# An eighth seven-product pair per layer, and two of its weight sums made by adding DMAs, in a two-layer mLSTM and retention encoder

## The chip, the cores and the metric

The kernel runs on one core of a Trainium2 chip. The metric is the device time of one execution in microseconds, lower is better; the time of the kernel before is the median of three runs.

## What is computed

Two layers, one after the other, each on 256 tokens of 2048 features in float32. A layer normalises its input, multiplies it by one wide weight matrix, and cuts the product into twelve parts. Two token mixers work on them: a bidirectional mLSTM and a bidirectional retention. Each mixer's result is normalised per head, multiplied by a SiLU gate, projected, and merged with the other under a sigmoid gate. An output projection and a residual add close the layer.

```python
def hybrid_layer(x, ...):
    h = rmsnorm(x, norm_w)
    proj = jnp.einsum('bsd,de->bse', h, w_in)
    (q_m, k_m, v_m, z_m, o_m, g_m, q_r, k_r, v_r, z_r, gate_m, gate_r) = jnp.split(proj, ...)
    ...
    h_m = jax.nn.sigmoid(split_heads(o_m, NH_M)) * h_m            # mLSTM scans, both directions
    u_m = head_rmsnorm(h_m, m_norm_w) * jax.nn.silu(z_m)
    ...
    u_r = head_rmsnorm(h_r, r_norm_w) * jax.nn.silu(z_r)          # retention scans, both directions
    mix = jax.nn.sigmoid(jnp.concatenate([gate_m, gate_r], axis=-1) + b_mix)
    y = (mix[..., :D_MODEL] * jnp.einsum('bse,ed->bsd', u_m, w_proj_m)
         + mix[..., D_MODEL:] * jnp.einsum('bse,ed->bsd', u_r, w_proj_r))
    return x + jnp.einsum('bsd,de->bse', y, w_out)
```

## The kernel before

**Weights and matmuls.** Tokens make two tiles of 128 (`t` = 0, 1), and 2048 features of a weight part make four blocks `b` of 512 columns. A weight block streams in from device memory in chunks of 128 x 1024 float32 (512 KB: two k-tiles of 128 rows by 512 columns). `wload` (line 251) puts a chunk into one of seven `raw` buffers, on the queue of the engine SP. Float32 products are made of three passes: `wsplit` has ScalarE round the chunk to `whi` (line 262) and VectorE subtract it, which leaves `wlo` (line 263); `mm3` then multiplies high by high, high by low and low by high (lines 271 to 273). `whi` and `wlo` come from a ring of twelve buffers, six pairs. A plain block (`gemm`, lines 332 to 351) is eight chunks, each used by 12 matmuls of 512 columns, six for each token tile.

**Side pairs.** `seven` (line 411) computes two blocks of one weight part together for both token tiles, in seven half-sized products where eight would do it plainly: the two token tiles by the two halves of the 2048 input features are one 2 x 2 matrix, the two halves of the features by the two blocks of columns the other. Each of the seven products takes four chunks (index `i`), six matmuls a chunk. The weight operand of a product is a quarter of the pair (`r11`, `r12`, `r21`, `r22`) or a sum of quarters. Product p5 uses r11+r12, p6 uses that plus r22 (kept in a big tile, `keep`), p7 uses r12+r22, and p4 uses the kept sum plus r21. Every one of these sums is a VectorE addition of 128 x 1024: `wsum` (line 268) for p5, p7 and p4, line 445 for p6. `middle` and `end` add the products together; `finish` (line 818) applies the gate function (a sigmoid or SiLU) to each 128 x 512 result and spills it to device memory. In each layer seven pairs are made so: the mLSTM output gate (`om`, two pairs), the merging gates (`gm` and `gr`, two pairs each), and blocks 0 and 1 of the retention's SiLU gate (`zr`).

**How the side work is woven in.** The items of the side pairs stand in one list, with weights (1.6 for a product with a VectorE sum, 0.5 without). After each chunk of a plain block, `side_chunk` puts in as many items as keep the list even over `20 * NCK` chunks, which is twenty blocks. `side_need` runs the list forward until a given result has been spilled. So through most of a layer TensorE alternates between a plain chunk and side products. Four places wait for side results: the blocks of `z_m` (name `zm`), the mLSTM projection (`pj`, with `gm`), the retention's gate and projection (with `gr`), and the next step.

**Spills and fetches.** A spill (line 99) is a DMA of 256 KB on the queue of the engine POOL. A fetch (line 105) is one on SP's queue, the same queue that the weights use, and it is in order: what stands behind a waiting issue waits too. A fetch lands in a 128 x 512 buffer of a ring of seven (`t512`), which the gate results (`c`, `z`), fetches and other temporaries share. Names in the trace end in `_b` for a fetched tile: `hm_b` is the mLSTM's output and `so_b` its sigmoid gate.

**The stage of `zm`.** For block `b` of four, `gated` fetches hm and om for both token tiles, multiplies them (VectorE) and sums the squares (ScalarE, which writes over `so_b`); meanwhile the plain block of `zm` runs; then the SiLU of it is multiplied in (`z<-hm_b,rstd_m,z`) and `um_chunk` transposes and splits the result, which is the left operand of `pj`.

**What sets the order.** The program is written in Python order and a list scheduler sorts each engine's instructions: `high_priority(offset=AHEAD)` (800) or `URGENT` (1600) lifts an instruction above those of the surrounding code. Each engine then runs its own list strictly in order. Functions given to `later` are generators that `run_later` steps, one step a chunk, from the third chunk on (`lead=3`).

Of the kernel before, what the change touches and what calls it, by code (L numbers as in the profile page):

```python
# [16 lines left out]
P = 128  # L17
D = 2048
# [43 lines left out]
def encoder_kernel(ctx: ExitStack, tc: tile.TileContext, x, x_t, positions, w_main, w_qk0, w_qk1, b_mgate, vecs, b_mix,  # L62
# [321 lines left out]
    def sums_of_operand(ht_hi, ht_lo, make_items):  # L384
# [24 lines left out]
        side_start(make_items(s_hi=s_hi, s_lo=s_lo, keep=bigt("keep", 4)), 20 * NCK)  # L409

    def seven(l, xop, s_hi, s_lo, keep, blk, finish):
# [17 lines left out]
        def p1(i):  # L429
            if i == 0:  # L430
                for name in "abcd":
                    st["ps_" + name] = bank("s" + name)
            load("r11", 0, i)
# [30 lines left out]
        def p2(i):  # L464
            if i == 0:
                for name in "acd":
                    st["ps_" + name] = bank("r" + name)
            load("r21", 0, HC + i)
            load("r22", 1, HC + i)
            product(st["ps_a"], lambda kt: xop(0, HK + kt), st["r21"], i, True, True)  # L470
# [293 lines left out]
    for l in range(DEPTH):  # L764
# [54 lines left out]
        def side_items(l=l, xop=xop, rs=rs, s_hi=None, s_lo=None, keep=None):  # L819
            def finish_with(kind, b0):  # L820
                def finish(t, n, src, own):
                    sg = t512(kind) if own is None else own
                    b = b0 + n
                    if kind in ("om", "zr"):
                        sca.activation(out=sg, in_=src, func=AF.Sigmoid if kind == "om" else AF.Silu, scale=rs[t])
                    else:
                        bm = row("bm")
                        mc = (0 if kind == "gm" else D) + b * NB
                        with tc.high_priority(offset=AHEAD):
                            nc.scalar.dma_start(out=bm, in_=b_mix[l:l + 1, mc:mc + NB].broadcast_to([P, NB]))  # L830
# [4 lines left out]
                return finish  # L835
            items = []
            for kind, base, b in (("om", B_O_M, 0), ("om", B_O_M, 2), ("gm", B_GATE, 0), ("gm", B_GATE, 2),
                                  ("zr", B_Z_R, 0), ("gr", B_GATE + NBLK, 0), ("gr", B_GATE + NBLK, 2)):
                items += seven(l, xop, s_hi, s_lo, keep, base + b, finish_with(kind, b))
# [52 lines left out]
        um = []  # L892
# [13 lines left out]
        def um_chunk(ev, b):  # L906
            um.append(transpose_split(ev, b, None, None, (l, V_MN)))

        for b in range(NBLK):
            side_need(("om", l, b, 1))  # L910
            side_need(("om", l, b, 0))
            hs = []
            ss_m = sm.tile([P, NT], F32, name="ss_m")
            later(gated, b, hs, ss_m)
            ps = gemm(xop, wmain(l, B_Z_M + b), "zm")
            while len(hs) <= NT:
                run_later()
            rstd_m = hs[NT]
            ev = []
            for t in range(NT):  # L920
                z = t512("z")
                sca.activation(out=z, in_=ps[t], func=AF.Silu, scale=rs[t])
                vec.scalar_tensor_tensor(out=z, in0=hs[t], scalar=rstd_m[:, t:t + 1], in1=z,
                                               op0=ALU.mult, op1=ALU.mult)
                ev.append(z)
            later(um_chunk, ev, b)
# [6 lines left out]
        for b in range(NBLK):  # L933
            ps = gemm(uop, wmain(l, B_PROJ_M + b), "pj")
            for t in range(NT):
                side_need(("gm", l, b, t))
                sg = fetch(("gm", l, b, t), "gm_b")
# [5 lines left out]
        def ur_chunk(b, zs):  # L943
            ev = []
            hrs = [fetch(("hr", l, 2 * b + k), "hr_b") for k in range(2)]
            for t in range(NT):
                z = fetch(("zr", l, b, t), "z_b") if zs is None else zs[t]
# [6 lines left out]
            if zs is None:  # L954
                yield
# [27 lines left out]
        for b in range(NBLK):  # L983
            if b == 2:
# [4 lines left out]
                later(y_chunk, None, 1)  # L989
            ps = gemm(rop, wmain(l, B_PROJ_R + b), "pj", lead=2)  # L990
            ev = []
            for t in range(NT):
                side_need(("gr", l, b, t))
                sg = fetch(("gr", l, b, t), "gr_b")
                ym = fetch(("ym", l, b, t), "ym_b")
# [184 lines left out]
```

## Time and profile before

| | |
|---|---|
| median of three runs | 2194.8 us (2194.19, 2194.8, 5458.12) |
| profiled execution, its own time | 2194.46 us |
| its span, first to last instruction | 2192.4 us |
| mean granted TensorE clock | 0.995 |
| TensorE (PE) busy | 2154.0 us, 98% |
| VectorE (DVE) busy | 1813.4 us, 83% |
| ScalarE (ACT) busy | 1304.3 us, 59% |
| data moved by DMA | 518.25 MB, mean 236 GB/s |

The profile's times come from one execution; 2.1 us of it lie outside the span. Busy shares are averages over the whole span. A timeline row gives start and duration of an instruction, and in square brackets how long the engine stood idle before it and what released it. Rows of stretches (the view by windows) give, for each engine, busy time and the count of instructions, and then the granted clock of TensorE, the busy share of the DMA engines and their GB/s.

### The profile page before, as it was taken

The numbers are of one execution on the slowest core, as the hardware profiler recorded it, in microseconds if no ns is written. First come the engines' busy times: TensorE is split into PE (matmuls) and PEld (weight loads), VectorE is DVE, ScalarE is ACT, GpSimd is POOL, SyncE is SP. The second block draws the span as 40 slices with busy tenths as digits, with TensorE's granted clock in tenths as the row PEclk, the third lists the DMA queues.
The fourth block names the chain that finished last, engine by engine and source line by source line (L and its number), as shares of the span: only waits on it lengthen the run. The fifth ranks groups of instructions, "written<-read, shape, count | busy, mean of one in ns | idle before, by whom it ended". The sixth has DMA issues, their size and how long they took to land.

```text
span 2192.4 us, 28486 instructions
## 1 busy us (share of the span) xinstructions
PE 2154.0 (98%) x10024; PEld 1809.9 (83%) x10024; DVE 1813.4 (83%) x2327; ACT 1304.3 (59%) x1627; POOL 66.9 (3%) x130
## 2 busy tenths in 40 slices
PE   7999999999999999999999999999999999999998
PEld 7988888888778888888899888888887788888887
DVE  6997898897898998985578778989978989889854
ACT  6745466656775656564457555665567656565543
POOL 0000000000000000000000000000000000000000
PEclk9999999999999999999999999999999999999999
DMA  8645577767777887887656456776777778878963
GB/s 277 213 150 190 191 236 236 229 229 241 241 241 264 280 283 258 271 295 276 221 168 208 164 185 210 236 234 216 240 247 239 255 255 292 280 252 277 326 223 125
DMA packets 161071, 518.25 MB, mean 236 GB/s; under 512 B 19616, under 2 KB 22176, under 8 KB 160928
## 3 DMA queue, kind: packets, MB, share of 16 engines
q1 hardware_dynamic: 143552, 471.98, 65.4%
q0 software_dynamic: 9600, 31.46, 3.6%
q10 hardware_dynamic: 7776, 13.00, 2.0%
q8 instruction: 78, 1.28, 0.2%
q14 instruction: 65, 0.53, 0.1%
HBM read 482.81 MB, written 33.55 MB: 236 GB/s over the span
## 4 chain that ended last, share of the span: by engine, by line
issue 48%; PE 42%; DVE 3%; DMA 3%; POOL 2%; ACT 1%; SPq 0%; ACTq 0%; POOLq 0%; DVEq 0%
PE pj L272 3%; PE pj L273 3%; PE pj L271 3%; DVE wlo L263 2%; PE vm L271 1%; PE vm L272 1%; PE wo L273 1%; PE wo L272 1%; PE wo L271 1%; PE vr L271 1%; PE vr L272 1%; PE qr L271 1%; PE vm L273 1%; PE qr L273 1%; PE vr L273 1%
## 5 line engine op out<-in xcount | busy, mean ns | idle before, releaser
L262 ACT CAST whi<-raw 128x1024 fp32r<-128x1024 f32 (+2 forms) x832 | 844.6, 1034 | 608.1 <-DVE raw L268 147.7
L263 DVE TENSOR_TENSOR wlo<-raw,whi 128x1024 fp32r<-128x1024 f32 (+2 forms) x832 | 981.0, 1200 | 214.7 <-ACT whi L262 200.1
L272 PE MATMUL pj<-wlo,u_hi 128*128 128x512 f32 x512 | 199.4, 390 | 0.6 <-DVE wlo L263 0.5
L271 PE MATMUL pj<-whi,u_hi 128*128 128x512 f32 x512 | 199.9, 391 | 0.0
L273 PE MATMUL pj<-whi,u_lo 128*128 128x512 f32 x512 | 199.3, 389 | 0.0
L262 ACT CAST whi<-keep 128x1024 fp32r<-128x1024 f32 x112 | 117.7, 1051 | 60.0 <-PE qr L272 12.8
L263 DVE TENSOR_TENSOR wlo<-keep,whi 128x1024 fp32r<-128x1024 f32 x112 | 136.4, 1218 | 15.7 <-ACT whi L262 15.1
L268 DVE TENSOR_TENSOR raw<-raw 128x1024 f32<-128x1024 f32 x112 | 136.4, 1218 | 0.8
L271 PE MATMUL qk<-whi,ht_hi 128*128 128x384 f32 (+2 forms) x320 | 113.7, 357 | 10.5 <-ACT whi L262 10.5
L272 PE MATMUL qk<-wlo,ht_hi 128*128 128x384 f32 (+2 forms) x320 | 113.4, 354 | 1.0 <-DVE wlo L263 1.0
L272 PEld LDWEIGHTS pj<-wlo,u_hi 128*128 128x128 f32 x512 | 96.1, 188 | 21.0 <-DVE wlo L263 1.5
L273 PE MATMUL qk<-whi,ht_lo 128*128 128x384 f32 (+2 forms) x320 | 113.0, 353 | 0.0
L273 PEld LDWEIGHTS pj<-whi,u_lo 128*128 128x128 f32 x512 | 96.1, 188 | 20.0
L271 PEld LDWEIGHTS pj<-whi,u_hi 128*128 128x128 f32 x512 | 96.0, 188 | 20.0 <-ACT whi L262 0.4
L272 PE MATMUL zm<-wlo,ht_hi 128*128 128x512 f32 x256 | 100.0, 391 | 1.0 <-DVE wlo L263 0.9
L271 PE MATMUL vm<-whi,ht_hi 128*128 128x512 f32 x256 | 100.3, 392 | 0.0
L273 PE MATMUL vm<-whi,ht_lo 128*128 128x512 f32 x256 | 100.2, 391 | 0.0
L271 PE MATMUL vr<-whi,ht_hi 128*128 128x512 f32 x256 | 100.1, 391 | 0.0
L271 PE MATMUL qr<-whi,ht_hi 128*128 128x512 f32 x256 | 100.1, 391 | 0.0
L272 PE MATMUL vm<-wlo,ht_hi 128*128 128x512 f32 x256 | 100.0, 391 | 0.0
L271 PE MATMUL zm<-whi,ht_hi 128*128 128x512 f32 x256 | 100.0, 392 | 0.0
L272 PE MATMUL vr<-wlo,ht_hi 128*128 128x512 f32 x256 | 99.8, 390 | 0.0
(313 smaller groups left out, 4664.6 us busy)
## 6 DMA issues: line engine op xcount, KB each, us to landing
raw<-in_w_main_dram SPq DMA_DIRECT2D x776, 512.0 KB, 5.0
raw<-in_w_qk_dram SPq DMA_DIRECT2D x48, 384.0 KB, 3.2
bm<-in_b_mix_dram ACTq DMA_DIRECT2D x32, 256.0 KB, 4.4
raw<-in_w_qk_dram SPq DMA_DIRECT2D x15, 400.0 KB, 5.2
hm<-hm POOLq DMA_DIRECT2D x16, 256.0 KB, 4.6
om<-c POOLq DMA_DIRECT2D x16, 256.0 KB, 3.5
hr<-hr POOLq DMA_DIRECT2D x16, 256.0 KB, 5.7
gm<-c POOLq DMA_DIRECT2D x16, 256.0 KB, 4.7
```

Of the source, the lines that this page charges most:

```text
L262: nc.scalar.copy(out=whi, in_=raw)
L263: nc.vector.tensor_tensor(out=wlo, in0=raw, in1=whi.bitcast(F32), op=ALU.subtract)
L268: nc.vector.tensor_tensor(out=dst, in0=a, in1=b, op=ALU.add)
L271: nc.tensor.matmul(out=ps, lhsT=xh, rhs=whi, start=first, stop=False)
L272: nc.tensor.matmul(out=ps, lhsT=xh, rhs=wlo, start=False, stop=False)
L273: nc.tensor.matmul(out=ps, lhsT=xl, rhs=whi, start=False, stop=last)
```

## The change

It has three parts. First, blocks 0 and 1 of the mLSTM's SiLU gate become an eighth side pair in each layer, spilled as `zm` and fetched where they are used. The loop over `zm` then has two plain blocks (2 and 3); beside each, `gated` runs for two heads, b and b-2, and fetches all of its four tiles before the first multiply. The side list is spread over `18 * NCK` chunks. Second, the sums of p7 and p4 leave VectorE: p1 loads r22 as `t3` and POOL issues a DMA that adds r12 from device memory into it; p6 issues one that adds r21 into the kept sum. These are 64 DMAs of 512 KB a layer, on POOL's queue. p5's sum now goes into the buffer of r12, since r11 is still read. Third, the bias rows of the merging gates (`bm`) are loaded by SP one step earlier, no longer by ScalarE's queue, and the fetches of `gm`, `ym` and `gr` stand ahead of the block that they gate.

```diff
-        side_start(make_items(s_hi=s_hi, s_lo=s_lo, keep=bigt("keep", 4)), 20 * NCK)
+        side_start(make_items(s_hi=s_hi, s_lo=s_lo, keep=bigt("keep", 4)), 18 * NCK)
...
             load("r12", 1, i)
-            load("r22", 1, HC + i)
+            load("t3", 1, HC + i)
+            with tc.high_priority(offset=AHEAD):
+                nc.gpsimd.dma_start(out=st["t3"], in_=wmain(l, blk + 1)(i), accum_op=ALU.add)
             product(st["ps_a"], lambda kt: xop(0, kt), st["r11"], i, True, True)
 
         def p5(i):
-            wsum(st["r11"], st["r11"], st["r12"])
-            product(st["ps_c"], lambda kt: sop(0, kt), st["r11"], i, True, True)
+            wsum(st["r12"], st["r11"], st["r12"])
+            product(st["ps_c"], lambda kt: sop(0, kt), st["r12"], i, True, True)
 
         def p6(i):
             with tc.high_priority(offset=AHEAD):
                 t2 = keep[:, i * CW:(i + 1) * CW]
-                nc.vector.tensor_tensor(out=t2, in0=st["r11"], in1=st["r22"], op=ALU.add)
+                nc.vector.tensor_tensor(out=t2, in0=st["r11"], in1=st["t3"], op=ALU.add)
             product(st["ps_b"], lambda kt: sop(1, kt), t2, i, True, True)
+            with tc.high_priority(offset=AHEAD):
+                nc.gpsimd.dma_start(out=t2, in_=wmain(l, blk)(HC + i), accum_op=ALU.add)
 
         def p7(i):
-            wsum(st["r12"], st["r12"], st["r22"])
-            product(st["ps_d"], lambda kt: sop(2, kt), st["r12"], i, True, True)
+            product(st["ps_d"], lambda kt: sop(2, kt), st["t3"], i, True, True)
...
         def p4(i):
             t2 = keep[:, i * CW:(i + 1) * CW]
-            wsum(t2, t2, st["r21"])
             product(st["ps_d"], lambda kt: xop(1, HK + kt), t2, i, True, True)
...
-            for w, fn in ((0.5, p1), (1.6, p5), (1.6, p6), (1.6, p7)):
+            for w, fn in ((0.5, p1), (1.6, p5), (1.6, p6), (0.5, p7)):
...
-            for w, fn in ((0.5, p2), (0.5, p3), (1.6, p4)):
+            for w, fn in ((0.5, p2), (0.5, p3), (0.5, p4)):
...
-            for kind, base, b in (("om", B_O_M, 0), ("om", B_O_M, 2), ("gm", B_GATE, 0), ("gm", B_GATE, 2),
+            for kind, base, b in (("om", B_O_M, 0), ("om", B_O_M, 2), ("zm", B_Z_M, 0), ("gm", B_GATE, 0), ("gm", B_GATE, 2),
...
         def gated(h, hs, ss):
-            for t in range(NT):
-                hv = fetch(("hm", l, h, t), "hm_b")
-                so = fetch(("om", l, h, t), "so_b")
+            ops = [(fetch(("hm", l, h, t), "hm_b"), fetch(("om", l, h, t), "so_b")) for t in range(NT)]
+            yield from pause(2)
+            for t in range(NT):
+                hv, so = ops[t]
                 vec.tensor_tensor(out=hv, in0=hv, in1=so, op=ALU.mult)
...
-        for b in range(NBLK):
+        for b in (2, 3):
             side_need(("om", l, b, 1))
             side_need(("om", l, b, 0))
-            hs = []
-            ss_m = sm.tile([P, NT], F32, name="ss_m")
-            later(gated, b, hs, ss_m)
-            ps = gemm(xop, wmain(l, B_Z_M + b), "zm")
...
+            for c in (b, b - 2):
+                hs = []
+                gs.append(hs)
+                later(gated, c, hs, sm.tile([P, NT], F32, name="ss_m"))
+                if c < 2:
+                    later(um_chunk, c, hs, None)
+            ps = gemm(xop, wmain(l, B_Z_M + b), "zm", lead=1)
...
         for b in range(NBLK):
+            for t in range(NT):
+                side_need(("gm", l, b, t))
+            sgs = [fetch(("gm", l, b, t), "gm_b", 60) for t in range(NT)]
             ps = gemm(uop, wmain(l, B_PROJ_M + b), "pj")
...
+            early = []
+            for t in range(NT):
+                if b < 2:
+                    early.append(fetch(("ym", l, b, t), "ym_b", 60))
+                    continue
+                early.append(fetch(("gr", l, b, t), "gr_b", 60))
             ps = gemm(rop, wmain(l, B_PROJ_R + b), "pj", lead=2)
```

Counted over the program, TensorE has 9964 matmul instructions where it had 10012, and POOL issues 256 DMAs where it issued 120: 128 adding ones and 8 spills of `zm` more.

The first place is SP's queue in the first layer's `zm` stage, from the fetches for the last plain block but one on. In a name such as `om_3_1` the digits are block and token tile; the last number is the program's own. Before, four fetches of one head stand together, or two by two, with sixteen weight loads between two heads:

```order
L105 DMA hm_b<-hm_2_0_2004 128x512
L105 DMA so_b<-om_2_0_4089 128x512
L105 DMA hm_b<-hm_2_1_2015 128x512
L105 DMA so_b<-om_2_1_4095 128x512
L251 DMA raw<-in_w_main_dram 128x1024 x16
L105 DMA hm_b<-hm_3_0_2246 128x512
L105 DMA so_b<-om_3_0_4092 128x512
L251 DMA raw<-in_w_main_dram 128x1024
L105 DMA hm_b<-hm_3_1_2257 128x512
L105 DMA so_b<-om_3_1_3761 128x512
```

Now the fetches for heads 3 and 1 stand within thirteen rows:

```order
L105 DMA so_b<-om_3_0_3898 128x512
L105 DMA hm_b<-hm_3_1_2257 128x512
L105 DMA so_b<-om_3_1_3551 128x512
L105 DMA hm_b<-hm_1_0_1830 128x512
L251 DMA raw<-in_w_main_dram 128x1024
L105 DMA so_b<-om_1_0_3012 128x512
L251 DMA raw<-in_w_main_dram 128x1024
L105 DMA hm_b<-hm_1_1_1841 128x512
L251 DMA raw<-in_w_main_dram 128x1024
L105 DMA so_b<-om_1_1_2757 128x512
L251 DMA raw<-in_w_main_dram 128x1024 x2
```

What moved: eight fetches of two heads and two of `z_b` behind them now stand where four stood, with five weight loads among them.

The second place is VectorE at the end of the same stage, between the last plain block of `zm` and the start of `pj`. Before, the two multiplies of head 3 (`hm_b<-hm_b,so_b`) have two `wlo` splits behind each:

```order
L119 SCALAR_TENSOR_TENSOR z<-hm_b,rstd_m,z 128x512 x2
L268 TENSOR_TENSOR keep<-keep,raw 128x1024
L263 TENSOR_TENSOR wlo<-keep,whi 128x1024
L119 TENSOR_TENSOR hm_b<-hm_b,so_b 128x512
L263 TENSOR_TENSOR wlo<-raw,whi 128x1024 x2
L119 TENSOR_TENSOR hm_b<-hm_b,so_b 128x512
L263 TENSOR_TENSOR wlo<-raw,whi 128x1024 x2
```

Now the last of four multiplies stands between the two gate products of head 3, and the splits for the next matmuls behind it:

```order
L263 TENSOR_TENSOR wlo<-raw,whi 128x1024
L119 SCALAR_TENSOR_TENSOR rstd_r<-rs_a,rs_r 128x16
L119 SCALAR_TENSOR_TENSOR z<-hm_b,rstd_m,z 128x512
L119 TENSOR_TENSOR hm_b<-hm_b,so_b 128x512
L119 SCALAR_TENSOR_TENSOR z<-hm_b,rstd_m,z 128x512
L263 TENSOR_TENSOR wlo<-raw,whi 128x1024
L119 TENSOR_SCALAR rs_a<-ss_m 128x2
L263 TENSOR_TENSOR wlo<-raw,whi 128x1024 x2
```

What moved: the multiplies of two heads and their statistics now come in the one place where those of one head came.

The third place is POOL's queue in the same stage, where `t3`'s additions are line 439 and the kept sum's are line 452. Before, it holds spills alone:

```order
L99 DMA om_2_1_4095<-c_4084 128x512
L99 DMA hr_4_4561<-hr 128x512
L99 DMA hr_5_4610<-hr 128x512
L99 DMA gm_1_1_4681<-c_4671 128x512
L99 DMA hr_6_4929<-hr 128x512
```

Now the adding DMAs stand among them:

```order
L99 DMA zm_1_1_4379<-c_4372 128x512
L439 DMA raw<-in_w_main_dram 128x1024
L99 DMA zm_0_0_4625<-c_4618 128x512
L99 DMA zm_1_0_4628<-c_4619 128x512
L99 DMA zm_0_1_4631<-c_4620 128x512
L439 DMA raw<-in_w_main_dram 128x1024
L452 DMA keep<-in_w_main_dram 128x1024
```

What moved: a chunk that used to be ready when SP's load had landed is now ready when a second DMA behind it on POOL's queue has landed too.

## Rows read from the trace of the kernel before

**Rows 1.** The page, section 1: busy us (share of the span) xinstructions of each engine.
```profile
PE 2154.0 (98%) x10024; PEld 1809.9 (83%) x10024; DVE 1813.4 (83%) x2327; ACT 1304.3 (59%) x1627; POOL 66.9 (3%) x130
```

**Rows 2.** Stretches by windows: length; PE, PEld, DVE, ACT, POOL busy; clock, DMA share, GB/s.
```profile
288.00:513.00 225.00, 225.00 (x1056) 188.55 (x1055) 197.40 (x207) 137.09 (x167) 7.60 (x14) 1.00 0.71 233
513.00:673.00 160.00, 152.92 (x689) 125.87 (x688) 138.10 (x176) 109.46 (x143) 4.88 (x9) 0.98 0.74 245
1595.00:1754.00 159.00, 152.15 (x691) 124.25 (x690) 136.89 (x175) 108.94 (x143) 4.88 (x9) 1.00 0.73 245
700.00:750.00 50.00, 50.00 (x222) 41.42 (x221) 45.28 (x44) 29.74 (x31) 2.72 (x5) 1.00 0.81 270
813.00:1011.00 198.00, 197.84 (x902) 164.18 (x901) 170.97 (x187) 118.86 (x135) 7.60 (x14) 1.00 0.85 287
```

**Rows 3.** Short stretches by windows, same columns: one behind a gap, two with full DMA engines.
```profile
579.00:584.00 5.00, 5.00 (x13) 3.95 (x14) 4.97 (x9) 4.72 (x6) 0.00 (x0) 0.55 0.39 124
780.00:785.00 5.00, 5.00 (x24) 4.14 (x23) 4.79 (x5) 2.48 (x3) 0.00 (x0) 1.00 0.97 381
1000.00:1005.00 5.00, 5.00 (x24) 4.14 (x23) 2.01 (x3) 2.11 (x2) 0.00 (x0) 1.00 1.04 407
```

**Rows 4.** What PE waited for over the span: us in total, times, longest us.
```profile
PE qk L271 <- ACT whi L262: 10.5, 2, 8.5
PE sd L272 <- DVE wlo L263: 8.4, 4, 4.6
PE ra L272 <- DVE wlo L263: 4.0, 4, 1.8
```

**Rows 5.** Timeline, SP, VectorE, ScalarE and PE around the one long gap of the `zm` stage.
```profile
568.64 0.46 SPq L105 DMA_DIRECT2D so_b<-om  x1
569.84 1.10 SPq L105 DMA_DIRECT2D so_b<-om  x1
571.03 8.16 SPq L251 DMA_DIRECT2D raw<-in_w_main_dram  x2
573.37 0.69 DVE L119 TENSOR_TENSOR hm_b<-hm_b,so_b 128x512 f32<-128x512 f32 x1 [2.72 <-DMA so_b<-om]
573.85 0.39 PE L271 MATMUL sd<-whi,s_hi 128*128 128x512 f32 x1
576.18 0.69 DVE L119 TENSOR_TENSOR hm_b<-hm_b,so_b 128x512 f32<-128x512 f32 x1 [2.12 <-DMA so_b<-om]
576.91 0.63 ACT L119 ACTIVATE so_b<-hm_b 128x512 f32<-128x512 f32 x1 [2.09 <-DVE hm_b L119]
577.58 1.21 DVE L263 TENSOR_TENSOR wlo<-raw,whi 128x1024 fp32r<-128x1024 f32 x1
578.85 0.79 PE L272 MATMUL sd<-wlo,s_hi 128*128 128x512 f32 x1 [4.61 <-DVE wlo L263]
```

**Rows 6.** The page, section 5: groups of instructions, busy, mean ns of one, idle before.
```profile
L262 ACT CAST whi<-raw 128x1024 fp32r<-128x1024 f32 (+2 forms) x832 | 844.6, 1034 | 608.1 <-DVE raw L268 147.7
L263 DVE TENSOR_TENSOR wlo<-raw,whi 128x1024 fp32r<-128x1024 f32 (+2 forms) x832 | 981.0, 1200 | 214.7 <-ACT whi L262 200.1
L268 DVE TENSOR_TENSOR raw<-raw 128x1024 f32<-128x1024 f32 x112 | 136.4, 1218 | 0.8
```

**Rows 7.** DMA issues: out<-in, queue, count, KB each, median us from issue to landing.
```profile
raw<-in_w_main_dram SPq DMA_DIRECT2D x776, 512.0 KB, 5.0
hm<-hm POOLq DMA_DIRECT2D x16, 256.0 KB, 4.6
so_b<-om SPq DMA_DIRECT2D x16, 256.0 KB, 6.1
hr_b<-hr SPq DMA_DIRECT2D x16, 256.0 KB, 6.8
y_b<-y SPq DMA_DIRECT2D x8, 256.0 KB, 9.4
```

**Rows 8.** What SP's queue waited for with weight loads: us, times, longest.
```profile
SPq L251 <- DVE wlo L263: 1402.2, 678, 10.8
```

More of the change, by code (lines that the diff above doesn't have):

```diff
@@ L408, in sums_of_operand, with seven @@
             yield
-        side_start(make_items(s_hi=s_hi, s_lo=s_lo, keep=bigt("keep", 4)), 20 * NCK)
-    def seven(l, xop, s_hi, s_lo, keep, blk, finish):
+        side_start(make_items(s_hi=s_hi, s_lo=s_lo, keep=bigt("keep", 4)), 18 * NCK)
+    def seven(l, xop, s_hi, s_lo, keep, blk, finish, early):
         def sop(i, kt):
@@ L820, in finish_with, with early @@
             def finish_with(kind, b0):
+                bms = {}
+                def early(n):
+                    if kind in ("gm", "gr"):
+                        bms[n] = row("bm")
+                        mc = (0 if kind == "gm" else D) + (b0 + n) * NB
+                        nc.sync.dma_start(out=bms[n], in_=b_mix[l:l + 1, mc:mc + NB].broadcast_to([P, NB]))
                 def finish(t, n, src, own):
@@ L823, in finish @@
                     b = b0 + n
-                    if kind in ("om", "zr"):
+                    if kind in ("om", "zm", "zr"):
                         sca.activation(out=sg, in_=src, func=AF.Sigmoid if kind == "om" else AF.Silu, scale=rs[t])
                     else:
[L827 to L830, printed above, removed]
+                        bm = bms[n]
                         vec.scalar_tensor_tensor(out=sg, in0=src, scalar=rs[t], in1=bm, op0=ALU.mult,
@@ L834, in finish @@
                     spill((kind, l, b, t), sg)
-                return finish
+                return finish, early
             items = []
-            for kind, base, b in (("om", B_O_M, 0), ("om", B_O_M, 2), ("gm", B_GATE, 0), ("gm", B_GATE, 2),
+            for kind, base, b in (("om", B_O_M, 0), ("om", B_O_M, 2), ("zm", B_Z_M, 0), ("gm", B_GATE, 0), ("gm", B_GATE, 2),
                                   ("zr", B_Z_R, 0), ("gr", B_GATE + NBLK, 0), ("gr", B_GATE + NBLK, 2)):
-                items += seven(l, xop, s_hi, s_lo, keep, base + b, finish_with(kind, b))
+                items += seven(l, xop, s_hi, s_lo, keep, base + b, *finish_with(kind, b))
             return items
@@ L904, in gated, with um_chunk @@
             hs.append(rstd_m)
-        def um_chunk(ev, b):
-            um.append(transpose_split(ev, b, None, None, (l, V_MN)))
-        for b in range(NBLK):
+        def um_chunk(b, hs, zs):
+            ev = []
+            if zs is None:
+                zs = [fetch(("zm", l, b, t), "z_b") for t in range(NT)]
+                yield from pause(2)
+            for t in range(NT):
+                z = zs[t]
+                vec.scalar_tensor_tensor(out=z, in0=hs[t], scalar=hs[NT][:, t:t + 1], in1=z, op0=ALU.mult,
+                                         op1=ALU.mult)
+                ev.append(z)
+            yield
+            um[b] = transpose_split(ev, b, None, None, (l, V_MN))
+            yield
+        for b in (2, 3):
             side_need(("om", l, b, 1))
             side_need(("om", l, b, 0))
-            hs = []
-            ss_m = sm.tile([P, NT], F32, name="ss_m")
-            later(gated, b, hs, ss_m)
-            ps = gemm(xop, wmain(l, B_Z_M + b), "zm")
[L916 to L919, printed above, removed]
+            side_need(("zm", l, b - 2, 1))
+            side_need(("zm", l, b - 2, 0))
+            gs = []
+            for c in (b, b - 2):
[5 more added lines that the diff above has]
+            ps = gemm(xop, wmain(l, B_Z_M + b), "zm", lead=1)
+            zs = []
             for t in range(NT):
@@ L922, in encoder_kernel @@
                 sca.activation(out=z, in_=ps[t], func=AF.Silu, scale=rs[t])
[L923 to L926, printed above, removed]
+                zs.append(z)
+            while len(gs[0]) <= NT:
+                run_later()
+            later(um_chunk, b, gs[0], zs)
         rstd_r = sm.tile([P, NT * NH_R], F32, name="rstd_r")
@@ L945, in ur_chunk @@
             hrs = [fetch(("hr", l, 2 * b + k), "hr_b") for k in range(2)]
+            if zs is None:
+                zs = [fetch(("zr", l, b, t), "z_b") for t in range(NT)]
+                yield from pause(2)
             for t in range(NT):
-                z = fetch(("zr", l, b, t), "z_b") if zs is None else zs[t]
+                z = zs[t]
                 for k in range(2):
@@ L993, in encoder_kernel @@
                 side_need(("gr", l, b, t))
-                sg = fetch(("gr", l, b, t), "gr_b")
-                ym = fetch(("ym", l, b, t), "ym_b")
+                sg = fetch(("gr", l, b, t), "gr_b") if b < 2 else early[t]
+                ym = fetch(("ym", l, b, t), "ym_b") if b >= 2 else early[t]
                 vec.tensor_tensor(out=sg, in0=ps[t], in1=sg, op=ALU.mult)
```

12 lines of the change are left out of this document (7 added, 5 removed).

## The prediction

> **What bounds the kernel now.** I read the page's busy line first: TensorE (PE) is busy 98% of the span, VectorE 83%, ScalarE 59% [rows 1]. A share over the whole span can hide a stage with another limit, so the view by windows came next. From 288 to 513 us and from 813 to 1011 us of the first layer PE is busy for the whole stretch, at full clock, while VectorE is at 88% and 86% [rows 2]. In the stage of `zm` (513 to 673, and 1595 to 1754 in the second layer) PE stands idle 7.1 and 6.9 us [rows 2]. The reader should see two things in these rows. VectorE, which the change relieves, is close behind PE but not what ends the time; and idle time that could be recovered in the touched stages is 13.9 us. PE's waits say the same in another way: it waits 8.4 us in all for `wlo` of side products (`sd`) and 4.0 us for `ra` [rows 4].
>
> The timeline shows how such a wait is made [rows 5]. The last of four fetches is issued at 569.84, its multiply on VectorE starts at 576.18, and behind this multiply in VectorE's list stands the `wlo` split that PE needs at 573.85. PE is idle for 4.61 us, and the clock then falls: in the next 5 us PE does 13 matmuls at a granted clock of 0.55, the lower level (1.2 GHz), where 22 fit at the higher (2.4 GHz) [rows 2, 3].
>
> **What the change removes.** The eighth pair takes 28 groups of half-products where two plain blocks take 32: 4 chunks x 6 matmuls = 24 of 512 columns less in a layer, 48 in all, as the counts of the program show. In 700 to 750 us 222 such matmuls fill 50 us, so one is 0.2252 us [rows 2]. 48 x 0.2252 = **10.8 us** saved, since PE is what ends the time there.
>
> VectorE loses 56 of its sums of 1.218 us in a layer [rows 6] and gets 4 sums for p5, 4 for p6 and 12 splits for the new pair's sums in their place, where the plain blocks had 16 splits and the pair has 28. That is 56 x 1.218 = 68 us less against some 24 us more. I cost this relief at nothing: in the side stages PE is already busy 100% [rows 2], so VectorE's time has nowhere to go. If VectorE were the bound, 44 us a layer would be at stake; the full PE rows exclude it.
>
> The idle 13.9 us of the two `zm` stages is tied to the old order of fetches. I count all of it as removed, and the new waits separately. Removed: 10.8 + 13.9 = **24.7 us**, 1.1% of the time. This is an upper bound on the gain, and lies well within 2%.
>
> **What it adds: three fetches in a row.** At the end of the second plain `zm` block the order shows the fetches of two heads where one head's stood. All fetches, gate results and `c` tiles share the seven buffers of `t512`. The fetch of om(3,1) can be issued only when a transposed `z` is free; that of om(1,0) goes into a buffer that ScalarE's square of the first product releases; that of om(1,1) waits for the next square. So three fetches come one behind another. One link takes 6.3 us from issue to multiply (569.84 to 576.18), then to the end of ScalarE's square at 577.54 (576.91 + 0.63), 7.7 us together [rows 5]. Three links are 23.1 us. VectorE's list has the last multiply ahead of the splits that `pj` and the side products need, so one split of 1.2 us comes on top [rows 6]: 24.3 us. In the meantime PE has, by the order, 42 matmuls between the transposes that free the first buffer and the matmuls behind the blocked splits: 42 x 0.2252 = 9.5 us. The stall is 24.3 - 9.5 = 14.8 us. A lower end is one link more under cover, 14.8 - 7.7 = 7 us. An upper end is that the two weight loads which stand between the fetches on SP's queue cost as in the trace, where two issues took 8.16 us [rows 5]: 23 us. I take 14.8, since each wait named here is in the order, and 2.1 us more for the lower clock behind a long gap ((22 - 13) x 0.2252 [rows 2, 3]), less the one of before. Two layers: 2 x 14.8 + 2 x 2.1 - 2.1 = **+31.7 us**.
>
> **What it adds: the adding DMAs.** The trace has no such DMA. Below, the nearest row is POOL's spill of half the size, 4.6 us; the load of the same 512 KB is 5.0 us; above, a read of the target and one of the source, in turn, are 2 x 5.0 = 10 us [rows 7]. I take 5.0, the row of the same size and place. What it does to PE: from the release of a `raw` buffer to PE's use of the product of p6 there are, by the order, 69 to 120 matmuls, median about 89, which is 15.5 to 27 us, median 20. In this time SP must issue the load (it waits for a release before 678 of 776 loads and so follows it at once [rows 8], but may stand behind another load, half of 8.16 us [rows 5]: I take 3.5), the load lands (5.0), the addition lands (A), VectorE makes the kept sum (1.22), ScalarE and VectorE split it (1.03 + 1.20) [rows 6, 7]: 12 + A. With A = 5 that is 17 us, and of 32 such chains in a layer only the few shortest are late, by 1 us or so each: 5 us a layer, **+10 us**. With A = 10 it is 22 us and more than half are late by some 2.5 us: an estimate of 50 us a layer, +100 us. The fourth sum (r21 into `keep`) has the whole of `middle` and p2, p3 between issue and use and costs nothing unless POOL's queue is late.
>
> The Trainium skill ("Collectives: The Full Stack", section "The bandwidth ceiling: the fold count and why AG ≠ RS ≠ AR") says that a DMA which adds reads two sources through the same ring and delivers at half the rate of a copy. By it the term would be the upper end, an estimate of +100 us instead of +10; no row here shows an addition, so it decides nothing yet.
>
> **What else it adds.** At the retention's gate the fetch of `hr_b` takes 6.8 us against a spill of `gr` just ahead; `y_b` takes 9.4 us and now stands behind `gr_b` and weight loads right before its transposes [rows 7]. Bounds are 0 (hidden as before) and one late fetch each of about 5 us a layer; I take 2.5 each, **+10 us** in two layers.
>
> **Sum.** 2194.46 (profiled execution; the median, 2194.8, is 0.3 above it) - 24.7 + 31.7 + 10 + 10 = 2221.5, say **2222 us**: the saved matmuls are real, and the new waits cost more than they save.
>
> **The rivals.**
>
> - *The fetches are absorbed.* If VectorE, with 44 us a layer less to do, runs the splits far enough ahead, the chain of three fetches starts earlier and the ring of six pairs covers it. For: the ring holds six pairs, 72 matmuls or 16 us. Against: the multiplies stand ahead of the splits in VectorE's list, and before, with one head's fetches, the gap was already 5 us. The price of the new waits falls to some 5 us for the additions: 2194.5 - 24.7 + 5 = 2175 us; with half of the old gaps left, 2185.
> - *The additions are slow.* A chain of 12 + 10 us is longer than the median window of 20 us, and 64 additions a layer read twice put 64 x 2 x 0.524 MB on DMA engines. In 813 to 1011 us they have a share of 0.85 at 287 GB/s, and stretches of 5 us are full at 381 to 407 GB/s [rows 2, 3]. The layer's additions spread over 785 us are 43 GB/s read once, 85 twice: 330 or 372 GB/s, near full. Time: 2222 + 90 = 2312 us; it goes over 2238 us (2% over 2194.5) from A of about 6 us. For it: nothing hides an addition from p6 but the window. Against: the load of equal size takes 5.0 us.
> - *The relief counts.* VectorE would be the bound, and 44 us a layer less of it gives 88 us: 2106 us. The full PE rows of the side stages speak against it; only 38.4 us of idle PE time exist in the whole span (2192.4 - 2154.0 [rows 1]).
>
> A gain or a loss of 2% is about what a measurement of this kernel can tell from no change.
>
> **Chances.** Waits as summed, 2195 to 2238: 0.45. Absorbed, 2165 to 2195: 0.30. Additions slow, over 2238: 0.23. Relief counts, under 2150: 0.02. Range: leaving out about 0.05 below and 0.12 above gives **2172 to 2280 us**; the likeliest case alone has 2200 to 2238. Faster by over 2%: 0.02; within 2%: 0.75; slower by over 2%: 0.23.
>
> **What the profile after would show.** If the saving is right, PE's matmul count is 48 lower and the full stretches keep 0.2252 us a matmul. If the fetch chain is right, PE's waits have 10 to 20 us in each layer at the start of `pj` behind `wlo`, VectorE's idle time there ends on `so_b`, and ACT's squares stand between three `so_b` landings some 7 us apart. If the additions fit, their median landing is near 5 us and waits of `keep` or `t3` splits on the DMA stay under 10 us a layer; at 8 us or more the second rival holds. The forecast is wrong if the `zm` stage has less idle PE time than the 7 us of before (the first rival), or if the lost time lies evenly over all the side products rather than at the start of `pj` and the two fetches named (the second).

## The result

The changed kernel takes **2499.6 us** (median of four runs, 2493.3 to 2509.4) against 2194.5 us: 1.14 times as long, 95% interval 1.135 to 1.145. One of the four runs of the kernel before took 5458.12 us; nothing here explains it, and the ratio leaves it out. The forecast was 2222 us, with a range to 2280. The slow additions were one of the rivals, at 2312 us, and even that was too low by 188 us.

The page and the DMA issues of the kernel after, which answer to [rows 1, 6, 7] (for instructions: busy, mean ns | idle before and releaser; for DMAs: KB, median us to landing):

```profile
PE 2244.1 (90%) x9976; PEld 1855.0 (74%) x9976; DVE 1742.9 (70%) x2269; ACT 1315.4 (53%) x1641; POOL 185.8 (7%) x266
q0 software_dynamic: 28672, 100.68, 18.0%
L449 DVE TENSOR_TENSOR keep<-raw 128x1024 f32<-128x1024 f32 x64 | 78.3, 1223 | 298.2 <-DMA raw<-in_w_main_dram 298.2
L268 DVE TENSOR_TENSOR raw<-raw 128x1024 f32<-128x1024 f32 x64 | 78.2, 1222 | 78.4 <-DMA raw<-in_w_main_dram 77.6
raw<-in_w_main_dram SPq DMA_DIRECT2D x784, 512.0 KB, 5.4
raw<-in_w_main_dram POOLq DMA_DIRECT2D x64, 512.0 KB, 8.6
keep<-in_w_main_dram POOLq DMA_DIRECT2D x64, 512.0 KB, 9.5
```

VectorE's busy time fell by 70 us, as the change meant it to (the forecast's sum had 88). But it now stands idle for 298 us ahead of the kept sum of p6 (line 449), and what ends the wait is the addition into `t3`. An addition lands after 8.6 us (median), not 5.0. PE, at 98% before, is at 90%. The 78 us ahead of p5's sum (line 268) are not the additions' doing: with no addition and no sum of p7 and p4 (a run shown below) they are 78.6 us too.

The stretches that were full in [rows 2], in the kernel after (busy times of PE, PEld, DVE, ACT, POOL; clock, DMA share, GB/s):

```profile
288.00:513.00 225.00, 198.74 (x864) 163.04 (x863) 154.08 (x165) 114.95 (x136) 19.96 (x27) 0.93 0.79 232
813.00:1011.00 198.00, 162.82 (x664) 131.06 (x663) 124.65 (x129) 95.05 (x102) 17.06 (x23) 0.90 0.84 252
```

The loss lies all over the side stages, not at one place. PE has 26 and 35 us of idle in them and the mean clock fell to 0.93 and 0.90. Over the span, PE's idle grew from 38.4 to 247.5 us (+209). Its busy time, 10.8 us less of which were due to the missing matmuls, grew from 2154.0 to 2244.1 (so +101, which goes with the lower clock). 209 + 101 - 11 = 299 us, which is the growth of the span (2491.6 - 2192.4).

One of these waits, in the timeline of the kernel after (start, duration, idle before and releaser):

```profile
334.11 7.70 SPq L251 DMA_DIRECT2D raw<-in_w_main_dram  x4
340.24 1.22 DVE L263 TENSOR_TENSOR wlo<-raw,whi 128x1024 fp32r<-128x1024 f32 x1
341.74 0.89 POOL L439 DMA_DIRECT2D raw<-in_w_main_dram  x1 [3.79 <-DVE wlo L263]
349.61 1.23 DVE L449 TENSOR_TENSOR keep<-raw 128x1024 f32<-128x1024 f32 x1 [8.15 <-DMA raw<-in_w_main_dram]
350.75 1.22 DVE L263 TENSOR_TENSOR wlo<-raw,whi 128x1024 fp32r<-128x1024 f32 x1
352.02 0.80 PE L272 MATMUL vr<-wlo,ht_hi 128*128 128x512 f32 x1 [6.84 <-DVE wlo L263]
```

SP issues the load of `t3` at 334.11, the first of the four; it lands at 340.5. POOL issues the addition at 341.74 (its row names a split of VectorE, which ended at 341.46, as what released it), and it lands at 349.58. VectorE, with nothing to do since 341.5, starts the kept sum 0.03 us later. Behind it in its list stands a split for a product that has nothing to do with the pair (`vr`), and PE has been waiting for that one for 6.84 us.

### The profile page after: what moved, and what is told of

The parts are those of the page before. It is cut to its first block, busy times and chain, and to the rows that moved or that the text cites. A ratio compares the mean times of both kernels' runs of the same rounds, so it can differ in the third digit from the quotient of the medians.

```text
span 2491.6 us, 28863 instructions
## 1 busy us (share of the span) xinstructions
PE 2244.1 (90%) x9976; PEld 1855.0 (74%) x9976; DVE 1742.9 (70%) x2269; ACT 1315.4 (53%) x1641; POOL 185.8 (7%) x266
## 3 DMA queue, kind: packets, MB, share of 16 engines
q0 software_dynamic: 28672, 100.68, 18.0%
## 5 line engine op out<-in xcount | busy, mean ns | idle before, releaser
L262 ACT CAST whi<-raw 128x1024 fp32r<-128x1024 f32 (+2 forms) x840 | 856.3, 1034 | 646.8 <-PE pj L272 110.0
L449 DVE TENSOR_TENSOR keep<-raw 128x1024 f32<-128x1024 f32 x64 | 78.3, 1223 | 298.2 <-DMA raw<-in_w_main_dram 298.2
L262 ACT CAST whi<-keep 128x1024 fp32r<-128x1024 f32 x128 | 134.4, 1050 | 149.7 <-DVE keep L449 89.9
L263 DVE TENSOR_TENSOR wlo<-keep,whi 128x1024 fp32r<-128x1024 f32 x128 | 155.9, 1218 | 3.6 <-ACT whi L262 2.3
L268 DVE TENSOR_TENSOR raw<-raw 128x1024 f32<-128x1024 f32 x64 | 78.2, 1222 | 78.4 <-DMA raw<-in_w_main_dram 77.6
L439 POOL DMA_DIRECT2D raw<-in_w_main_dram x64 | 56.3, 880 | 808.4 <-DMA raw<-in_w_main_dram 422.4
L272 PE MATMUL qr<-wlo,ht_hi 128*128 128x512 f32 x256 | 101.7, 397 | 3.6 <-DVE wlo L263 3.6
L273 PE MATMUL vr<-whi,ht_lo 128*128 128x512 f32 x256 | 103.7, 405 | 0.0
L273 PE MATMUL qr<-whi,ht_lo 128*128 128x512 f32 x256 | 100.8, 394 | 0.0
```

Source lines behind the costliest of these rows:

```text
L262: nc.scalar.copy(out=whi, in_=raw)
L263: nc.vector.tensor_tensor(out=wlo, in0=raw, in1=whi.bitcast(F32), op=ALU.subtract)
L268: nc.vector.tensor_tensor(out=dst, in0=a, in1=b, op=ALU.add)
L272: nc.tensor.matmul(out=ps, lhsT=xh, rhs=wlo, start=False, stop=False)
L273: nc.tensor.matmul(out=ps, lhsT=xl, rhs=whi, start=False, stop=last)
L439: nc.gpsimd.dma_start(out=st["t3"], in_=wmain(l, blk + 1)(i), accum_op=ALU.add)
```

## The experiments: what makes the 305 us

**All sums back on VectorE, the eighth pair kept.**

```diff
-                nc.gpsimd.dma_start(out=st["t3"], in_=wmain(l, blk + 1)(i), accum_op=ALU.add)
...
+            wsum(st["r12"], st["r12"], st["t3"])        # p7
...
-                nc.gpsimd.dma_start(out=t2, in_=wmain(l, blk)(HC + i), accum_op=ALU.add)
...
+            wsum(t2, t2, st["r21"])                     # p4
```

With them p5's sum goes back to the buffer of r11, and the side items' weights to 1.6.

> The eighth pair, the new fetches and the new order of the changed kernel stay; the sums of p7 and p4 go back to VectorE, no adding DMA. Theory A (the addition into t3 is a link of about 9 us ahead of p6 and p7 that the seven raw buffers can't cover, so its 298 us of VectorE idle before the kept sum are the loss): 2190 to 2225 us. Theory B (the eighth pair and the chain of fetches in the zm stages make the loss): above 2350 us. Theory C (POOL's in-order queue: a kept-sum addition at its head waits for a split and holds the t3 addition behind it): as A. Theory D (DMA engines too full): as A.

2249.5 us, ratio 1.026 (1.0245 to 1.0279). So the additions make 250 us of the loss, and the eighth pair with its fetches 55. Theory B falls as the main cause. Theory A has the place, not the size: 250 us, where it took the whole 298 us of VectorE's idle for the loss.

**Only one of the two additions.** The kernel as changed, with p4's sum on VectorE (64 additions into `t3`), and with p7's on VectorE (64 into the kept sum).

> As changed, but the sum of p4 is back on VectorE: 64 adding DMAs, all into t3. A: nearly all of the loss stays, 2430 to 2500 us. C: the head of POOL's queue is free, most of the loss goes, under 2300 us. D: half of the added traffic goes, about half of the loss, 2330 to 2380 us. B: about 2500 us.

> As changed, but the sum of p7 is back on VectorE: 64 adding DMAs, all into the kept sum, which is used only after middle, p2 and p3. A: 2190 to 2240 us. C: the queue still waits at its head, but only spills stand behind it: 2200 to 2300 us. D: half of the loss, 2330 to 2380 us. B: about 2500 us.

2540.7 and 2247.5 us, some 40 and 8 us above theory A's ranges. The whole loss of the additions comes with the addition into `t3`; the one into the kept sum costs nothing against VectorE's sum. The rows of the second kernel show it:

```profile
keep<-in_w_main_dram POOLq DMA_DIRECT2D x64, 512.0 KB, 8.4
L447 DVE TENSOR_TENSOR keep<-raw 128x1024 f32<-128x1024 f32 x64 | 78.2, 1222 | 1.4
```

Its additions land as late, 8.4 us, but VectorE waits 1.4 us in all. POOL's order (theory C) falls, since the loss stays with POOL's queue free of kept sums. So does the traffic (D): half of the additions keep the whole loss, the other half cost nothing, and in the two stretches above the DMA engines' share was 0.79 and 0.84 on average, not full.

**The kernel before with both additions.**

```diff
+            load("t3", 1, HC + i)
...
+                nc.gpsimd.dma_start(out=st["t3"], in_=wmain(l, blk + 1)(i), accum_op=ALU.add)
...
+                nc.gpsimd.dma_start(out=t2, in_=wmain(l, blk)(HC + i), accum_op=ALU.add)
```

> The kernel before with seven pairs, its fetches and its spread over 20 blocks, and only the two sums made by adding DMAs (112). A and D: 7/8 of the loss, 2194 + 0.875 x 300 = 2440 to 2460 us. B: about 2200 to 2230 us.

2445.6 us, +254, with 56 additions into `t3` in place of 64. The loss needs neither the eighth pair nor the new fetches.

**Plain copies in place of the additions.**

```diff
-                nc.gpsimd.dma_start(out=st["t3"], in_=wmain(l, blk + 1)(i), accum_op=ALU.add)
+                nc.gpsimd.dma_start(out=st["t3"], in_=wmain(l, blk + 1)(i))
```

> As changed, with the same 128 DMAs on POOL's queue in the same places and with the same waits, but plain copies that overwrite instead of adding, so the weight sums of p7 and p4 are wrong. A1 (the addition itself is dear, 8.6 us against some 5.5 us for a copy of 512 KB): VectorE's idle before the kept sum falls from 298 us to under 150 us, time 2330 to 2400 us. A2 (any second DMA behind the load does it, the addition as such costs nothing): landing stays at 8 to 9 us, 2460 to 2510 us.

2383.5 us. Its rows:

```profile
q0 software_dynamic: 28672, 100.68, 12.0%
L449 DVE TENSOR_TENSOR keep<-raw 128x1024 f32<-128x1024 f32 x64 | 78.3, 1224 | 185.7 <-DMA raw<-in_w_main_dram 185.5
raw<-in_w_main_dram POOLq DMA_DIRECT2D x64, 512.0 KB, 6.3
```

Both causes count. A second DMA behind the load costs 134 us (2383.5 - 2249.5; 135 against the run below that has neither DMA nor sums, 2248.1), though it only copies; that it adds costs another 116. VectorE's idle is 186 us, more than the 150 that A1 named, and the time lies in A1's range. Queue 0 moves the same 100.68 MB in the two kernels. In the run with all sums on VectorE the same queue has the same 128 spills alone; they took 3.8% of a span of 2244.6 us, 85 us (a mean over the 16 DMA engines). The copies take 12.0% of 2374.2 less 85, which is 200 us, and the additions 18.0% of 2491.6 less 85, which is 363: 1.8 times as much for the same bytes. The Trainium skill ("Collectives: The Full Stack", section "The bandwidth ceiling: the fold count and why AG ≠ RS ≠ AR") says of the adding step of a collective that it needs two source reads and so runs at half the rate of the copying one. The trace comes near it in engine time (1.8 times); in landing it is 8.6 against 6.3 us, 1.4 times.

**Three ways to give the addition more time.** p6 and p7 one chunk later (p6 and p7 of i behind p5 of i+1); nine raw buffers with five pairs of `whi` and `wlo`; `t3` of chunk i+1 loaded and added to ahead of p5 of i.

```diff
-            for w, fn in ((0.5, p1), (1.6, p5), (1.6, p6), (0.5, p7)):
+            for w, fn, i in ((0.5, p1, j), (1.6, p5, j), (1.6, p6, j - 1), (0.5, p7, j - 1)):
```

> As changed, all 128 additions kept, but p6 and p7 of chunk i stand behind p1 and p5 of chunk i+1, so that the addition into t3 has two to three items and as many plain chunks longer (some 8 to 12 us) before VectorE asks for it. A: VectorE's idle before the kept sum falls under 100 us, 2270 to 2350 us. If the traffic of the additions is the cause: 2450 to 2510 us. If the seven raw buffers now run out instead: the loads stall and the time stays over 2400 us with the waits moved to VectorE's splits on DMA.

> As changed, with nine raw buffers and five pairs of whi and wlo in the same space (seven and six before). If the addition's window is set by the raw buffers: VectorE's idle before the kept sum falls from 298 us to under 200 us, 2380 to 2440 us. If the traffic or POOL's queue sets it: 2490 to 2530 us.

> The run of 2249 us (eighth pair, all sums on VectorE) with nine raw buffers and five pairs of whi and wlo: the other half of the run of 2563 us. If more raw buffers shorten the wait for the additions, the shorter ring alone must cost more than 63 us here: 2330 us or more. If raw buffers don't matter for the additions: 2290 to 2330 us, the difference between additions and VectorE's sums staying at 250 us.

```diff
         def p5(i):
+            if i + 1 < HC:
+                sum3(i + 1)        # load of t3 for i+1, and its addition
```

> As changed, all 128 additions kept, but t3 of chunk i+1 is loaded and added to ahead of p5 of chunk i. The chain from VectorE's release of a raw buffer to the kept sum is 15 us in the run as changed (load 5.4, issue 0.7, addition 8.6). By the order, VectorE has 8.7 us of work of its own in that time as changed, 9.1 and 8.5 in the runs of 2503 and 2563 us (where nothing was won), and 11.6 here: short of 15 us by 405, 402, 428 and 300 us in sum over the 64 chains. If VectorE's own work between release and sum is the window: its idle before the kept sum falls by some 100 us to about 200, 2390 to 2440 us. If the additions cost in another way (traffic, POOL): 2480 to 2520 us.

2503.2, 2562.8, 2267.0 and 2450.5 us. The later use and the additional buffers bring nothing. The third run is the control for the second, and is under both of its expectations: the shorter ring alone costs some 17 us, so with nine raw buffers the additions cost 296 us, not less than 250.

Matching each load, addition and kept sum of the kernel after (64 chains, medians) shows what the wait is made of: VectorE's release of a raw buffer to the load's issue 0.0 us, the load 5.4, to POOL's issue 0.7, the addition 8.6, to the kept sum 0.0; 14.9 in all, of which VectorE is idle 5.3. Both ends of this chain stand in VectorE's own list, with only some 9 us of its own work between, and neither of the first two edits changed that (8.7 us as changed, 9.1 and 8.5 in these runs, by the order). The sum one chunk ahead has 11.6 us and takes 49 us less, but misses its range of 2390 to 2440, and VectorE's idle fell only to 269 us. So the direction is shown and the size isn't.

Two of these edits also made a new wait, which the expectation of the later use named as its third case, though for VectorE. Used later, or loaded earlier, a raw buffer is held longer, which fits this wait, though no run tests it. ScalarE's rounding waited 86 us for SP's weight loads in the kernel after; with the later use it is 295 us, and one chunk ahead 206. The rows of the two runs:

```profile
L262 ACT CAST whi<-raw 128x1024 fp32r<-128x1024 f32 (+2 forms) x840 | 855.1, 1034 | 786.3 <-DMA raw<-in_w_main_dram 294.7
L262 ACT CAST whi<-raw 128x1024 fp32r<-128x1024 f32 (+2 forms) x840 | 859.5, 1034 | 750.6 <-DMA raw<-in_w_main_dram 205.8
```

In the second the addition also landed later (9.0 us). No run separates the new wait from the late landing. Over all runs with a DMA into `t3`, the time lost rises with VectorE's idle ahead of the kept sum, except for the later use (the run without is 2248.1 for the copies, 2191.8 for the kernel before, 2267.0 with nine buffers, and 2249.5 for the others):

| run | VectorE's idle ahead of the kept sum, us | us lost against the nearest run without these DMAs |
|---|---|---|
| plain copies | 186 | 135 |
| one chunk ahead | 269 | 201 |
| as changed | 298 | 250 |
| kernel before with both additions | 306 | 254 |
| additions into `t3` only | 323 | 291 |
| nine raw buffers | 351 | 296 |
| later use | 253 | 254 |

## The experiments: what the eighth pair costs

**Free sums.** The kernel before and the kernel as changed, without the sums of p7 and p4.

> The kernel before with the sums of p7 and p4 left out (p7 takes r12 alone, p4 the kept sum without r21): what a free addition would bring with seven pairs. If VectorE is not the bound, as the full PE rows say: 2185 to 2196 us. If VectorE's relief counts (136 us of its time gone): under 2150 us.

> As changed, with the two sums left out altogether (p7 takes r22 alone, p4 the kept sum without r21): no adding DMA and no addition on VectorE in their place, which is the price of a free addition. A, with VectorE not the bound: 2225 to 2250 us, like the run with VectorE's sums. If VectorE's load is the bound of the eighth pair: 2170 to 2195 us.

2183.6 us (0.994, interval 0.993 to 0.996), just under the first expectation, and 2248.1, in the first one's range. With seven pairs, a free addition would bring 12 us, 0.6%: that is all that VectorE's relief can be worth there. With the eighth pair as changed it brings nothing (2248.1 against 2249.5, where the side items' weights differ too), since something else ends the time.

**The fetch chain.** In the run with all sums on VectorE the end of the `zm` stage reads as forecast. Windows, then SP's and VectorE's timeline:

```profile
600.00:660.00 60.00, 44.99 (x175) 33.50 (x174) 52.20 (x77) 34.76 (x52) 1.62 (x3) 0.83 0.78 262
640.00:650.00 10.00, 5.16 (x11) 2.73 (x9) 10.00 (x24) 7.63 (x14) 0.00 (x0) 0.50 0.78 245
```

```profile
631.43 0.32 SPq L105 DMA_DIRECT2D so_b<-om  x1
638.14 0.32 SPq L105 DMA_DIRECT2D so_b<-om  x1
644.47 0.32 SPq L105 DMA_DIRECT2D so_b<-om  x1
...
636.67 0.69 DVE L119 TENSOR_TENSOR hm_b<-hm_b,so_b 128x512 f32<-128x512 f32 x1 [2.71 <-DMA so_b<-om]
639.58 0.69 DVE L119 TENSOR_TENSOR hm_b<-hm_b,so_b 128x512 f32<-128x512 f32 x1 [0.69 <-DMA so_b<-om]
642.61 0.69 DVE L119 TENSOR_TENSOR hm_b<-hm_b,so_b 128x512 f32<-128x512 f32 x1
647.39 0.69 DVE L119 TENSOR_TENSOR hm_b<-hm_b,so_b 128x512 f32<-128x512 f32 x1
```

The three fetches of `so_b` are 6.7 and 6.3 us apart, the second and the third issued right behind the square that frees their buffer. PE is idle 15.0 us from 600 to 660, which is all its idle time in 513 to 673, and at the lower level of the clock (0.50, which is 1.2 GHz) in 640 to 650, with 11 matmuls. To loosen the chain, two waiting steps are taken per chunk of the `zm` blocks, first with the sums on VectorE and then without them:

```diff
-            ps = gemm(xop, wmain(l, B_Z_M + b), "zm", lead=1)
+            ps = gemm(xop, wmain(l, B_Z_M + b), "zm",
+                      before=lambda ck: [run_later() for _ in range(2 if ck else 0)])
```

> All sums on VectorE and the eighth pair, as in the run of 2249 us, but in the two zm blocks two waiting steps are taken per chunk, so that the fetches of the second pair of heads are issued some 10 us or more earlier. If the chain of three fetches makes 15 us of idle and 5 us of low clock per layer: 2205 to 2220 us. If the 55 us come from VectorE's load of the eighth pair: 2240 to 2260 us.

> As changed, with the sums of p7 and p4 left out altogether (p7 takes r22 alone, p4 the kept sum without r21) and two waiting steps per chunk in the zm blocks. If VectorE's time for sums makes what is left of the eighth pair's loss (44 us) once the fetch chain is loosened: 2170 to 2200 us. If not: 2230 to 2245 us, and the loss lies in the splits and waits of the pair itself.

2239.3 and 2223.5 us. Loosening the chain is worth 10 us with VectorE's sums and 25 without (2248.1 - 2223.5); neither run is where its theory put it. With the sums, PE's idle in 513 to 673 us falls from 15.0 to 10.1 us only. What is left without sums can be named, in PE's waits (us in total, times, longest; the wait of `qk`, 10.2 us, is also in [rows 4]):

```profile
PE tr L235 <- DVE z L119: 10.6, 2, 5.5
PE zm L272 <- DVE wlo L263: 8.4, 8, 2.1
PE zr L271 <- DVE u_lo L119: 7.9, 4, 3.4
PE tr L235 <- DMA y_b<-y: 7.0, 2, 3.6
```

**Old fetches, packing.** The kernel before with the eighth pair and the looser `zm` stage only, spread over 18 and over 20 blocks; the same over 18 without the two sums; and the kernel before with its seven pairs packed into 16 blocks.

```diff
-            for kind, base, b in (("om", B_O_M, 0), ("om", B_O_M, 2), ("gm", B_GATE, 0), ...
+            for kind, base, b in (("om", B_O_M, 0), ("om", B_O_M, 2), ("zm", B_Z_M, 0), ("gm", B_GATE, 0), ...
```

> The kernel before with the eighth pair, the zm stage of the changed kernel with two waiting steps per chunk, and the spread over 18 blocks; the bias rows, the fetches of gm, ym and gr, and the retention's gate stay as before, all sums on VectorE. If the moved fetches and bias loads make the 44 us that are left in the run of 2239 us: 2190 to 2205 us. If the eighth pair itself makes them (side products packed into 18 blocks, more splits for PE's time): 2230 to 2245 us.

> The same with the side list spread over 20 blocks as before. If the packing into fewer blocks makes the loss, this spreads it wider but ends later, where it is forced: within 10 us of the spread over 18. If the late side products are waited for: 10 to 30 us slower than that.

> The run of the eighth pair with the fetches and bias loads of before (2253 us), with the sums of p7 and p4 left out. If the moved fetches make the gaps that are left in the run of 2224 us (transposes waiting for hr_b and y_b, 3 to 6 us each): 2190 to 2205 us. If they lie in the eighth pair's order itself: 2220 to 2235 us.

> The kernel before with its seven pairs packed into 16 blocks (1.53 side items per plain chunk, as the eighth pair's 1.56 over 18; before 1.23). If dense side products starve PE (each split pair feeds six matmuls there, twelve in a plain chunk): 2215 to 2240 us. If density is harmless: 2190 to 2205 us.

2252.8, 2250.4, 2215.7 and 2199.6 us. The moved fetches and bias loads are not the loss (2252.8 against 2239.3 with sums, 2215.7 against 2223.5 without), nor is the spread (2250.4 against 2252.8), and packing alone costs 6 to 7 us. The first and the third run lie outside both of their ranges. With the old fetches the sums cost 37 us (2252.8 - 2215.7) where they cost 12 with seven pairs; with the new fetches and the looser `zm` stage it is 16 (2239.3 - 2223.5, the weights differing too). So with the eighth pair VectorE's time can begin to count. Even with free sums the best run of the pair is 1.0% behind the kernel before (1.0081 to 1.0115). Its trace says what these last 21 us are: PE has 18 us more of idle time (56.1 against 38.4) and, with the 10.8 us of saved matmuls taken off, 14 us more of busy time, which goes with the lower mean clock (0.988). New gaps of up to 5 us stand at transposes that wait for a product with the fetched `zr` (9.6 us in all) and at side products that wait for a split (6.5 us at `sb`, 5.9 at `sc`). Why the eighth pair opens just these stays open.

**A version that might gain.** The addition that is hidden, on the kernel before:

```diff
+                nc.gpsimd.dma_start(out=t2, in_=wmain(l, blk)(HC + i), accum_op=ALU.add)
...
-            wsum(t2, t2, st["r21"])
```

> The kernel before with one change: the sum of p4 is made by the adding DMA into the kept tile (56 of them), whose result is used only after middle, p2 and p3. If the additions are hidden there, as in the run of 2248 us, and VectorE's relief is worth at most the 12 us of the run without both sums: 2184 to 2196 us. If POOL's queue or the traffic makes it dear in this order: 2200 us or more.

2202.6 us, 1.0035 (1.0022 to 1.0048): 8 us slower, as the second expectation had it; whether POOL's queue or the traffic does it isn't shown. VectorE has 56 us less to do and PE waits more, not less, for `sd` (11.2 us in all against 8.4 in [rows 4]). No version here that makes all the sums beats the kernel before.

## Why the prediction was wrong, step by step

- **"I take 5.0, the row of the same size and place."** This step failed first. An addition took 8.6 and 9.5 us, near the upper bound of 10. The load's row was the wrong one: a copy of that size on the same queue takes 6.3 us, and adding costs the rest. The rule that the prediction quotes from the Trainium skill, as deciding nothing yet, pointed the right way (the numbers are with the plain copies).
- **"From the release of a raw buffer to PE's use ... median 20."** This is the step that sank the forecast, and it is why even the rival was too low: by its reckoning A = 8.6 would cost some 75 us, between 10 at A = 5 and 100 at A = 10, and the runs gave 250. The chain was not at fault. The 3.5 us for standing behind another load measured 0.0, so from release to the end of the split it is some 18.4 us (14.9 + 1.22 + 1.03 + 1.20), less than the 12 + 8.6 of the sum, and would fit the window of 20. The window was measured in PE's work. But VectorE releases the raw buffers, as [rows 8] say, and VectorE makes the kept sum, so the window is VectorE's own work between the two, some 9 us against a chain of 15. Such a wait comes in 51 of 64 chains. This window is read from the order; the one run that widened it, to 11.6 us, gained 49.
- **What is queued behind the wait** was counted for the product of p6 alone. VectorE runs in order, so its 298 us of idle hold back the splits of other products too, of plain blocks as well (`vr` in the timeline above).
- **The clock** was priced at 2.1 us for each long gap. Waits by the dozen brought it to 0.947 over the whole span: 101 us, a third of the loss.
- **The fourth sum "costs nothing unless POOL's queue is late"** held with eight pairs (2247.5 against 2249.5); with seven it cost 8 us.
- **VectorE's relief "at nothing"** held for the kernel as changed (0 us) and nearly with seven pairs (12 us); with eight pairs and other fetches or the looser `zm` stage it was 37 and 16 us.
- **The three fetches in a row** came in order and size: 14.8 us of idle in a layer forecast, 15.0 measured where the additions are away. The size is luck in part. The idle spreads over several waits of 1 to 4 us, not one, and loosening the chain took away 5 of the 15 us.
- **"What else it adds", 2.5 us each,** was too small: the transposes wait 3.6 us for `y_b` and 5.5 for `hr_b`'s product, and the start of `zr` for `u_lo` was not in the sum at all. With the clock behind these gaps the eighth pair came to +55 us, where the sum without the additions had +17 (2211.5). In its trace, which is 52 us longer than before, these are 43 us of idle and 20 us of busy time at a lower clock, less the 10.8.
- **Where the loss would lie:** evenly over the side products, the sign that the prediction set for its second rival. The traffic, the other half of that rival, was not the cause.
- **"2% is about what a measurement of this kernel can tell"** was too coarse: the ratios here have intervals of 0.3 to 1.0% from end to end.

## What to carry to other kernels

When work moves from an engine to a DMA, measure the time that covers the DMA in the list of the engine that waits for it, from the event which lets the DMA start to the wait; if that engine also causes the event, the work of the busiest engine is no measure of it. An in-order engine that waits holds back all that stands behind it, so here the price was 0.7 to 1.0 of its idle time, the lower clock of TensorE included. Before relieving an engine, leave the work out and time that: here it would have shown that 12 us were the most to be had from the relief.

## What the runs showed of the hardware

An adding DMA from device memory into on-chip memory took 1.8 times the engine time of a copy of the same bytes (363 against 200 us, a mean over 16 engines, for 128 of 512 KB) and landed after 8.6 us where the copy took 6.3 and SP's load 5.4. With TensorE's waits of up to 9 us, often repeated, went a mean granted clock of 0.947 and 101 us of added busy time beside 209 us of added idle.
